# Two stream waits in the gated delta heads of a three-layer kernel

## The chip, the cores and the metric

The kernel runs on one core of one Trainium2 chip. The metric is the device time of one launch in microseconds (us), the median of 3 runs. A core has five engines, each working through its own instructions in order and waiting at semaphores for the others: TensorE (PE, with PEld for its weight loads), VectorE (DVE), ScalarE (ACT), GpSimd (POOL) and SyncE (SP), which here only issues transfers. On-chip memory is SBUF; matrix products land in PSUM.

## The reference, cut to what matters

The program computes a gated delta layer with memory attention and a feed-forward layer, then a convolution layer, a sparse attention layer and two more feed-forward layers, on 512 positions of width 1024. Everything here happens in the first part, the gated delta rule with 8 heads of width 128:

```
q = l2norm(q) * 128**-0.5;  k = l2norm(k);  beta = sigmoid(b)
G = cumsum(g);  decay = exp(G_i - G_j) on and below the diagonal
lower = strictly lower part of beta * (k k^T) * decay
u, w = solve (I + lower) x = [v * beta, k * beta * exp(G)]
p = (q k^T) * decay
per chunk:  v_new = u - w S;  o = (q exp(G)) S + p v_new
            S = S * exp(G_last) + (k exp(G_last - G))^T v_new
o = rms_norm(o) * silu(z)
```

with q, k, v and z the columns of one projection of the normed input, and q, k and v passed through a causal convolution of width 4 and a silu.

## The kernel before, in words

The weights are multiplied in three passes (high x high, high x low and low x high halves of a float32 product, lines 230 to 232), so one projection of a head (128 columns) is 24 matmuls of 512 columns. Weights come from memory through SP's queue in the order of a list, ScalarE rounds them to a high half (L223), and GpSimd forms the low half of the heads' weights (L225).

A head h of the gated delta part is one Python generator, `gdn_head` (L657), and the projections of all heads, then those of the memory attention, are another (`projections`, `gdn_proj` L635). Both are run by the class `Mix` (L88): it keeps a clock and a list of streams, and always takes the stream of least rank that may run. A stream hands back a pair: the first number moves the clock on (estimated TensorE time), the second says for how long that stream steps aside. So `yield 0.0, 5` adds nothing; it lets the others emit up to 5 us of TensorE work before the stream goes on. Heads have ranks 0 to 7, the memory heads 20 and more, and the projections 40, so that they are what fills in. A stream can also hand back a condition. What `Mix` emits is a program order; a list scheduler of the language's runtime then takes it as priorities and fixes for each engine the order in which its instructions stand. That order is final: an engine that waits for one instruction waits with all that follow it.

A head's steps, with the names that the tables use:

- `gdn_proj`: products `wk`, `wq`, `wv`, `wz` of the head (L230 to L232); for k, q and v a scaled copy and three shifted products on VectorE (L644), then a silu on ScalarE (all of ScalarE's functions are recorded at L170); for z only the silu.
- Transposes of k, q, v into PSUM (`natk`, `natq`, `natv`, L668). Of k and q ScalarE takes squares (`sqk`, `sqq`) and VectorE sums (`ss`, L673); of v VectorE forms beta v (`bv`, L676).
- Norms and gates: a logarithm (`lr`), small columns `cs` on VectorE (L681 to L691, of which L685 and L686 form `aL`), two exponentials of them on ScalarE, and `kg`, k times a column (L693).
- Decays: for L and P, transposes of broadcast columns into PSUM (`pbL`, `pbP`, L699), VectorE's differences (`ddL`, `ddP`, L702), an exponential, products of keys and queries (`pkL`, `pkP`, L710) and the elementwise product (L711); for P also `eq` (L707).
- The solve of 16x16 blocks: a mask on GpSimd (`um`, L718), a reduction (`uc`, L720), then 15 steps of shuffle, product and difference (`br`, `xc`, L726 to L728) on VectorE.
- Two levels of combining (`pya`, `pza`, `pyb`, `pzb`, L751, and `py`, `pt`, L776 and L783), four chunks of the recurrence (`pc`, `po`, L796 to L815), a norm of the output (`pr`, `rs`) and its split into halves (`ym`).

Functions of ScalarE come in table sets. Logarithm and exponential share one that the kernel asks for at L162 (`lnexp`); the silu is in another. Where the order puts a function of another set next, a load (ACT_TABLE_LOAD) stands before it.

The steps of the prediction touch the loop at L663 to L677, the gates at L678 to L693 and the decays from L695 on.

Of the kernel before, what the change touches and what calls it, by code (L numbers as in the profile page):

```python
# [125 lines left out]
def body(ctx, tc, I, out, dump=None):  # L126
# [11 lines left out]
    def slot(name, dt=F32):  # L138
        return act.tile([P, S], dt, tag="s", name=name)
# [7 lines left out]
    def bank(name):  # L147
        return psg.tile([P, S], F32, tag="g", name=name)
# [16 lines left out]
    def af(o, i, func, **k):  # L165
        if func in (AF.Ln, AF.Exp):
            lnexp()
        elif func not in (AF.Copy, AF.Square):
            table[0] = func
        return A.activation(o, i, func, **k)  # L170
# [450 lines left out]
    def v4(t):  # L621
        return t.rearrange("p (c i) -> p c i", i=P)

    def bl(t, c):
        return t[:, c * P:(c + 1) * P]

    def cbc(col):
        return col.unsqueeze(2).to_broadcast([P, NB, P])
# [28 lines left out]
    def gdn_head(h):  # L657
# [5 lines left out]
        nat = {}  # L663
        for i, nm in enumerate("kqv"):
            t = kqv[nm]
            ps = bank(f"nat{nm}{h}")
            for c in range(NB):
                T.transpose(bl(ps, c), bl(t, c), ident)  # L668
            nat[nm] = ps
            if nm != "v":  # L670
                s2 = slot(f"sq{nm}{h}")
                af(s2, ps, AF.Square)
                V.tensor_reduce(ss[:, 4 * i:4 * i + 4], v4(s2), AX.X, ALU.add)  # L673
            else:
                bv = slot(f"bv{h}")
                V.tensor_tensor(v4(bv), v4(ps), cbc(beta[:, :, h]), ALU.mult)  # L676
            yield 0.43, 0  # L677
# [13 lines left out]
        V.tensor_scalar(ea, ea, -1.0, None, ALU.mult)  # L691
        kg = slot(f"kg{h}")
        V.tensor_tensor(v4(kg), v4(nat["k"]), cbc(ek), ALU.mult)  # L693

        mats = []  # L695
        for i, (nm, col, mv) in enumerate((("L", aL, kT), ("P", aP, qT))):
# [258 lines left out]
    for h in range(NH):  # L955
        mix.add(gdn_head(h), h)
# [841 lines left out]
```

## Time and profile before

| | |
|---|---|
| median of 3 runs | 2055.21 us (2054.76 to 2057.18) |
| the profiled execution | 2055.91 us, its span 2054.1 us |
| granted TensorE clock, mean | 0.992 |
| PE busy | 1982.7 us (97%) |
| DVE busy | 1543.8 us (75%) |
| ACT busy | 1036.7 us (50%) |
| POOL busy | 321.4 us (16%) |

Busy shares are of the whole span. The gated delta heads fill only the stretch from about 48 to 430 us, and a share over the span says little of it. "Idle before" is the time in which an engine stood still right ahead of an instruction; what is named behind the arrow ended it.

### The profile page before, as it was taken

What the parts mean: (1) busy time and instruction counts of PE and PEld (TensorE: products, weight loads), DVE (VectorE), ACT (ScalarE), POOL (GpSimd) and SP (SyncE); (2) the same over time, 40 slices, a digit from 0 to 9 for tenths busy, and PEclk for the clock granted to TensorE, in tenths of its full rate; (3) what the DMA queues carried; (4) which work ended last, traced back from release to release, by engine and by line L of the source; (5) the groups of instructions that cost most, each with busy time, mean ns of one, the idle gap of its engine ahead of it and who ended that gap; (6) DMA issues with size and microseconds to landing.
All of it is one profiled execution on the core that took longest, in us unless ns stands there. A gap on an engine that the chain in (4) does not pass through costs nothing.

```text
span 2054.1 us, 32051 instructions
## 1 busy us (share of the span) xinstructions
PE 1982.7 (97%) x12464; PEld 1695.7 (83%) x12464; DVE 1543.8 (75%) x2887; ACT 1036.7 (50%) x1734; POOL 321.4 (16%) x227
## 2 busy tenths in 40 slices
PE   7898889999999999998999999999999999999998
PEld 5777777878899988886589999888766678999987
DVE  5888888655989982597778999535888868998832
ACT  5545666553544452457754445434766645444522
POOL 3332433101100000148100000000333310000000
PEclk9999999999999999999999999999999999999999
DMA  5211111412233333233122333334100022323331
GB/s 149 62 52 52 52 52 62 142 55 81 79 107 104 103 113 97 81 92 103 42 93 93 113 101 109 106 95 116 52 22 22 21 65 77 116 93 114 106 99 63
DMA packets 204577, 172.45 MB, mean 84 GB/s; under 512 B 13250, under 2 KB 199243, under 8 KB 204425
## 3 DMA queue, kind: packets, MB, share of 16 engines
q1 hardware_dynamic: 197248, 163.85, 25.9%
q10 hardware_dynamic: 6152, 3.40, 0.6%
q0 software_dynamic: 1024, 3.15, 0.5%
q8 instruction: 98, 1.61, 0.3%
q14 instruction: 55, 0.44, 0.1%
HBM read 165.15 MB, written 2.10 MB: 81 GB/s over the span
## 4 chain that ended last, share of the span: by engine, by line
PE 81%; DVE 14%; ACT 2%; issue 1%; POOL 0%; DMA 0%; ACTq 0%; DVEq 0%; POOLq 0%
PE f L230 16%; PE f L231 16%; PE f L232 16%; PE ao L1676 2%; PE pT L1655 2%; DVE br L727 1%; DVE xc L728 1%; PE cv L1249 1%; PE p L232 1%; PE p L231 1%; PE p L230 1%; DVE dw L1277 1%; PE s L1568 1%; PE wo L231 1%; PE wo L230 1%
## 5 line engine op out<-in xcount | busy, mean ns | idle before, releaser
L225 DVE TENSOR_TENSOR f_l<-f_r,f_h 128x1024 fp32r<-128x1024 f32 (+2 forms) x88 | 101.2, 1151 | 166.8 <-ACT f_h L223 162.9
L223 ACT CAST f_h<-f_r 128x1024 fp32r<-128x1024 f32 (+2 forms) x88 | 87.1, 991 | 188.1 <-PE f L231 148.7
L1646 POOL TENSOR_SCALAR p<-p,dn 128x256 f32<-128x256 f32 (+2 forms) x64 | 72.8, 1142 | 120.5 <-DVE dn L1644 83.6
L170 ACT ACTIVATE p<-s,nm 128x512 f32<-128x512 f32 (+3 forms) x128 | 66.3, 528 | 34.8 <-DVE nm L1640 13.9
L1442 POOL CAST KB<-K 128x128 fp32r<-128x128 f32 x4 | 1.6, 410 | 464.6 <-ACT K L1418 464.6
L170 ACT ACT_TABLE_LOAD x45 | 57.7, 1283 | 12.8 <-DVE v L644 4.9
L359 DVE TENSOR_TENSOR f_s<-f_s,f 128x1024 f32<-128x1024 f32 x52 | 63.5, 1221 | 0.1
L225 POOL TENSOR_TENSOR p_a_l<-p_a_r,p_a_h 128x1024 fp32r<-128x1024 f32 x4 | 9.9, 2474 | 330.3 <-DMA p_a_r<-in_a_pw_w 315.4
L1640 DVE TENSOR_REDUCE nm<-s 128x1 f32<-128x512 f32 (+2 forms) x96 | 50.2, 547 | 7.4 <-PE s L1568 6.8
L354 ACT CAST f_q1h<-f 128x1024 fp32r<-128x1024 f32 x26 | 27.3, 1051 | 55.9 <-DVE f_q3l L355 54.9
L355 DVE TENSOR_TENSOR f_q1l<-f,f_q1h 128x1024 fp32r<-128x1024 f32 x26 | 31.9, 1225 | 25.4 <-ACT f_q1h L354 25.4
L1275 POOL TENSOR_TENSOR dw<-dw,dt 128x511 f32<-128x511 f32 (+29 forms) x30 | 43.7, 1456 | 28.6 <-ACT dt L170 26.8
L225 DVE TENSOR_TENSOR p_l<-p_r,p_h 128x1024 fp32r<-128x1024 f32 x20 | 30.6, 1536 | 18.2 <-ACT p_h L223 18.2
L1655 PEld LDWEIGHTS pT<-cst,p 128*128 128x128 f32 x320 | 36.0, 140 | 9.2 <-issue 4.2
L1676 PE MATMUL ao<-pt,vN 128*64 128x128 f32 (+3 forms) x256 | 42.6, 440 | 0.0
L354 ACT CAST f_q7h<-f 128x1024 fp32r<-128x1024 f32 x26 | 27.3, 1049 | 29.0 <-DVE f_q2l L355 26.6
L354 ACT CAST f_q2h<-f 128x1024 fp32r<-128x1024 f32 x26 | 27.3, 1052 | 27.9 <-issue 27.0
L1655 PE MATMUL pT<-cst,p 128*128 128x128 f32 x320 | 41.1, 274 | 0.2 <-DVE pt L1659 0.2
L727 DVE TENSOR_TENSOR br<-br,uc 128x4 f32<-128x4 f32 (+14 forms) x120 | 38.6, 322 | 2.5
L354 ACT CAST f_q6h<-f_s 128x1024 fp32r<-128x1024 f32 x26 | 27.4, 1052 | 25.6 <-DVE f_s L359 12.7
L354 ACT CAST f_q5h<-f_s 128x1024 fp32r<-128x1024 f32 x26 | 27.3, 1051 | 24.7 <-DVE f_s L359 23.8
L728 DVE TENSOR_TENSOR xc<-xc,br 128x4 f32<-128x4 f32 (+14 forms) x120 | 37.1, 309 | 2.7
(2420 smaller groups left out, 7977.0 us busy)
## 6 DMA issues: line engine op xcount, KB each, us to landing
f<-in_ffn_w_in SPq DMA_DIRECT2D x72, 512.0 KB, 3.9
f<-in_w_ffn_in SPq DMA_DIRECT2D x32, 512.0 KB, 3.5
f_r<-in_ffn_w_out SPq DMA_DIRECT2D x30, 512.0 KB, 3.4
p_r<-in_a_pw_w SPq DMA_DIRECT2D x20, 512.0 KB, 4.0
f_r<-in_w_ffn_out SPq DMA_DIRECT2D x14, 512.0 KB, 3.4
wo_r<-in_w_out SPq DMA_DIRECT2D x12, 512.0 KB, 3.4
f_r<-in_ffn_w_out SPq DMA_DIRECT2D x14, 384.0 KB, 3.0
wk_r<-in_gdn_w_in SPq DMA_DIRECT2D x8, 512.0 KB, 3.7
```

Of the source, the lines that this page charges most:

```text
L170: return A.activation(o, i, func, **k)
L223: A.copy(hi, raw)
L225: (G if idle else V).tensor_tensor(lo, raw, hi.bitcast(F32), ALU.subtract)
L230: T.matmul(ps, wh, xh, start=first, stop=False)
L231: T.matmul(ps, wh, xl, start=False, stop=False)
L232: T.matmul(ps, wl, xh, start=False, stop=last)
L354: A.copy(hi, raw)
L359: V.tensor_tensor(raws[o], raws[a], raws[b], ALU.add)
L727: V.tensor_tensor(br[:, :, 0:w], br[:, :, 0:w], uc[:, :, i:i + 1].to_broadcast([P, NB, w]), ALU.mult)
L1646: (V if br else G).tensor_scalar(pp[br, qb], pp[br, qb], den[:, br:br + 1], None, ALU.mult)
L1655: T.transpose(ps[:, off + (qb - kb) * P:off + (qb - kb + 1) * P], bl(pp[br, qb], kb), ident)
L1676: T.matmul(po[64 * i:64 * i + 64, kb * P:S], VN[br][:, kb * P + 64 * g:kb * P + 64 * g + 64], rhs, start=False, stop=j == 7)
```

## The change: two pairs of numbers

`gdn_head` hands control back twice more: ahead of the transposes of v, for 3.0, and behind `kg`, ahead of the decays, for 2.0. No instruction is named in it.

```diff
         for i, nm in enumerate("kqv"):
             t = kqv[nm]
+            if nm == "v":
+                yield 0.0, 3.0
             ps = bank(f"nat{nm}{h}")
...
         kg = slot(f"kg{h}")
         V.tensor_tensor(v4(kg), v4(nat["k"]), cbc(ek), ALU.mult)
+        yield 0.0, 2.0
```

Lines of the changed kernel stand 2 or 3 further down. The order in which instructions stand is another from the first head on. Counted over the whole program, ScalarE's order has 66 table loads before and 81 now. Of the 15 more, 3 stand up to the silu of head 0's z, 5 between it and that of head 1's z, then 1, 2, 3 fewer, 2, 4 and none for the heads 2 to 7, and 1 behind.

ScalarE, head 1, from the squares of its queries to the exponential of its decays, before:

```order
L162 ACT_TABLE_LOAD
L170 ACTIVATE lr1_736<-ss1_701,epst_86 128x8
L170 ACT_TABLE_LOAD
L170 ACTIVATE v1_681<-v1_681 128x512
L170 ACT_TABLE_LOAD
L170 ACTIVATE cs1_740<-cs1_740 128x4 x2
L223 CAST wz2_3328_0_h_967<-wz2_3328_0_r_966 128x1024
L170 ACTIVATE ddL1_756<-ddL1_756 128x512
```

and now:

```order
L162 ACT_TABLE_LOAD
L170 ACT_TABLE_LOAD
L170 ACTIVATE v1_666<-v1_666 128x512
L170 ACT_TABLE_LOAD
L170 ACTIVATE lr1_744<-ss1_686,epst_86 128x8
L223 CAST wz2_3328_0_h_927<-wz2_3328_0_r_926 128x1024
L170 ACT_TABLE_LOAD
L170 ACTIVATE cs1_748<-cs1_748 128x4 x2
L170 ACT_TABLE_LOAD
L170 ACTIVATE z1_762<-wz10_672 128x512
L170 ACT_TABLE_LOAD
L170 ACTIVATE ddL1_793<-ddL1_793 128x512
```

The silu of v stands ahead of the logarithm, the silu of z ahead of the exponential of the decays (before, it stood behind them), and six loads stand where there were three.

VectorE, where the products of head 2's values (`v2`) stand among the steps of head 1's solve (`br1`, `xc1`, counted down from 15 to 1), before:

```order
L726 STREAM_SHUFFLE br1_3_1041<-xc1_811 128x4x13
L727 TENSOR_TENSOR br1_3_1041<-br1_3_1041,uc1_809 128x4x13
L728 TENSOR_TENSOR xc1_811<-xc1_811,br1_3_1041 128x4x13
L726 STREAM_SHUFFLE br1_2_1069<-xc1_811 128x4x14
L785 TENSOR_SCALAR XU0_913<-pt0_2_1035 64x4x64
L644 SCALAR_TENSOR_TENSOR v2_1019<-wv20_965,vecs_88,v2_1019 128x511
L673 TENSOR_REDUCE ss2_1045<-sqk2_1051 128x4
L644 SCALAR_TENSOR_TENSOR v2_1019<-wv20_965,vecs_88,v2_1019 128x510
L673 TENSOR_REDUCE ss2_1045<-sqq2_1059 128x4
L644 SCALAR_TENSOR_TENSOR v2_1019<-wv20_965,vecs_88,v2_1019 128x509
L727 TENSOR_TENSOR br1_2_1069<-br1_2_1069,uc1_809 128x4x14
```

and now:

```order
L731 TENSOR_TENSOR xc1_849<-xc1_849,br1_4_1012 128x4x12
...
L729 STREAM_SHUFFLE br1_4_1062<-xc1_849 128x4x12
L730 TENSOR_TENSOR br1_4_1062<-br1_4_1062,uc1_847 128x4x12
L731 TENSOR_TENSOR xc1_849<-xc1_849,br1_4_1062 128x4x12
L644 SCALAR_TENSOR_TENSOR v2_994<-wv20_925,vecs_88,v2_994 128x511
L675 TENSOR_REDUCE ss2_1014<-sqk2_1020 128x4
L644 SCALAR_TENSOR_TENSOR v2_994<-wv20_925,vecs_88,v2_994 128x510
L675 TENSOR_REDUCE ss2_1014<-sqq2_1032 128x4
L644 SCALAR_TENSOR_TENSOR v2_994<-wv20_925,vecs_88,v2_994 128x509
L729 STREAM_SHUFFLE br1_3_1076<-xc1_849 128x4x13
```

The products of v stand a step and a third earlier, and the product `XU0` of the head before, which stood ahead of them, is gone from here.

TensorE, around the transposes of head 2's values and its first decays (`wk30` is the projection that fills in, `pc0_0` and `pt0_2` belong to head 0), before:

```order
L231 MATMUL wk30_1187<-u0_1l_174,wk3_1408_0_h_1027 128x512
L668 MATMUL natv2_1062<-cst_80,v2_1019 128x128 x4
L802 MATMUL pc0_0_1077<-bv0_449,XU0_913 128x128
L699 MATMUL pbL2_1096<-cst_80,cs2_1085 128x128 x4
L232 MATMUL wk30_1187<-u0_1h_173,wk3_1408_0_l_1028 128x512
L710 MATMUL pkL2_1107<-k2_880 128x128 x4
```

and now:

```order
L230 MATMUL wk30_1140<-u0_2h_182,wk3_1408_0_h_1006 128x512
L670 MATMUL natv2_1066<-cst_80,v2_994 128x128 x4
L786 MATMUL pt0_2_1103<-XU0_955,y0_2_1060 64x64 x4
L702 MATMUL pbL2_1113<-cst_80,cs2_1084 128x128 x4
L713 MATMUL pkL2_1125<-k2_864 128x128 x4
L805 MATMUL pc0_0_1132<-bv0_464,XU0_955 128x128
```

The transposes of v stand one row later, with two more matmuls of the filler ahead of them; nothing of 3 us has come in between, and `pbL` still follows closely, behind products of head 0. Over the heads 0 to 7 the row number of `natv` on TensorE went from 163, 266, 377, 502, 651, 778, 894, 1012 to 159, 261, 378, 501, 639, 756, 905, 1010, and that of `pbL` from 164, 267, 379, 503, 652, 779, 904, 1023 to 170, 273, 380, 506, 653, 774, 914, 1032.

## Rows read from the trace of the kernel before

**Rows 1.** Busy time of the engines in two stretches of the heads, in us.

```profile
core 0: us, PE busy (x) PEld busy (x) DVE busy (x) ACT busy (x) POOL busy (x), PEclk, DMA share, GB/s
60.00:340.00 280.00, 246.98 (x1374) 204.64 (x1372) 240.91 (x754) 159.56 (x237) 101.54 (x55) 0.96 0.18 53
340.00:400.00 60.00, 58.52 (x390) 51.96 (x391) 45.26 (x139) 32.38 (x62) 15.05 (x18) 0.97 0.35 121
```

**Rows 2.** The chain that ended last, 40 to 410 us: by line, then pieces.

```profile
by line: DVE br L727 7.5%; DVE xc L728 7.4%; DVE v L644 4.3%; DVE br L726 4.1%; DVE q L644 3.7%; issue 3.2%; ACT L170 3.1%; PE pkL L710 2.2%; PE wk L232 2.2%; PE wk L230 2.1%; PE wq L230 2.1%; PE wk L231 2.1%; PE wq L232 2.0%; DVE ss L673 2
...
86.66 0.64 ACT v L170
87.34 1.12 PE natv L668 x4
```

**Rows 3.** TensorE's waits, 60 to 400 us: total us, times, longest.

```profile
PE natv L668 <- ACT v L170: 8.6, 5, 4.0
PE pbL L699 <- DVE cs L686: 4.4, 2, 2.9
PE pbL L699 <- DVE cs L688: 2.0, 1, 2.0
PE natq L668 <- ACT q L170: 1.9, 1, 1.9
PE pkP L710 <- DVE kg L693: 1.3, 1, 1.3
```

**Rows 4.** VectorE's waits for these transposes, 50 to 350 us.

```profile
DVE bv L676 <- PE natv L668: 5.8, 3, 2.6
DVE ddP L702 <- PE pbP L699: 4.4, 4, 1.7
```

**Rows 5.** TensorE in order of time: start, us, [idle before <- releaser].

```profile
87.34 1.12 PE L668 MATMUL natv<-cst,v 128*128 128x128 f32 x4 [4.05 <-ACT v L170]
89.10 1.92 PE L710 MATMUL pkL<-k 128*128 128x128 f32 x8
...
124.62 0.66 PE L668 MATMUL natv<-cst,v 128*128 128x128 f32 x4 [2.34 <-ACT v L170]
126.06 1.16 PE L710 MATMUL pkL<-k 128*128 128x128 f32 x8
...
219.18 0.44 PE L699 MATMUL pbL<-cst,cs 128*128 128x128 f32 x1 [2.91 <-DVE cs L686]
```

**Rows 6.** ScalarE's table loads in the whole span: count, busy us, mean ns.

```profile
L170 ACT ACT_TABLE_LOAD x45 | 57.7, 1283 | 12.8 <-DVE v L644 4.9 <-DVE q L644 4.0 <-DVE k L644 2.4
L162 ACT ACT_TABLE_LOAD x21 | 26.9, 1283 | 1.1 <-PEq L1788 0.7
```

**Rows 7.** ScalarE in order of time, heads 1 and 2.

```profile
87.30 1.28 ACT L170 ACT_TABLE_LOAD   x1
88.60 0.30 ACT L170 ACTIVATE cs<-cs 128x4 f32<-128x4 f32 x2
...
96.10 0.60 ACT L170 ACTIVATE z<-wz 128x512 f32<-128x512 f32 x1
...
123.94 0.63 ACT L170 ACTIVATE v<-v 128x512 f32<-128x512 f32 x1
...
127.55 0.20 ACT L170 ACTIVATE cs<-cs 128x4 f32<-128x4 f32 x1
127.66 1.03 ACT L223 CAST wz_h<-wz_r 128x1024 fp32r<-128x1024 f32 x1
129.72 0.64 ACT L170 ACTIVATE ddL<-ddL 128x512 f32<-128x512 f32 x1 [1.03 <-DVE ddL L702]
```

**Rows 8.** VectorE in order of time, head 2.

```profile
119.00 0.41 DVE L785 TENSOR_SCALAR XU<-pt 64x256 f32<-64x256 f32 x1
...
127.97 0.68 DVE L693 TENSOR_TENSOR kg<-natk,cs 128x512 f32<-128x512 f32 x1
128.57 1.12 DVE L702 SCALAR_TENSOR_TENSOR ddL<-pbL,cs,tab 128x128 f32<-128x128 f32 x4
...
136.66 1.03 DVE L720 TENSOR_REDUCE uc<-um 128x64 f32<-128x512 f32 x1 [0.67 <-POOL um L718]
```

## The prediction

> **What bounds the kernel now.** I read the busy times by stretch first, because the page's shares are means over stages with different limits and the change acts in one stage alone. From 60 to 340 us, where the heads follow one another, TensorE is busy for 246.98 of 280 us and VectorE for 240.91, so TensorE stands still for 33 us and no engine is full; from 340 to 400 us TensorE is busy for 58.52 of 60 [rows 1]. Behind that stretch the change moves nothing but names. VectorE's 240.91 understates it: of a solve step only the product and the difference count, not the shuffle.
>
> The second view is the chain that ended last. Between 40 and 410 us its largest lines are the solve steps on VectorE (7.5 + 7.4 + 4.1% of 370 us, 70 us over 120 steps, so about 0.6 us a step), then VectorE's products for v and q; at a head's start it crosses over, by the silu of v on ScalarE, to the transposes of v on TensorE [rows 2]. So the stage is a loop of engines that wait for each other: VectorE's solve of one head delays the values of the next, TensorE stands at their transposes, and VectorE then waits for what TensorE could not do.
>
> The third view, TensorE's waits, gives the size of what the change is aimed at: 8.6 us for v, 4.4 + 2.0 us for the columns of the decays, 1.3 us for `kg`, together 16.3 us; the queries cost 1.9 [rows 3]. The same stops appear on VectorE as 5.8 and 4.4 us [rows 4]. The longest, 4.05 us in head 1, costs more than itself: behind it the eight matmuls of `pkL` took 1.92 us, in head 2 they took 1.16 [rows 5], which is the lower of the clock's two levels (1.2 against 2.4 GHz) after the engine had stood still.
>
> **The change, part by part.** No instruction is named in it, but ScalarE's order has 15 loads more, 15 x 1.283 = 19.2 us at the duration of the 66 [rows 6]. ScalarE has room: 159.56 of 280 us busy [rows 1]. What counts is where a load stands in a chain.
>
> *Heads 0 and 1.* Eight of the 15 stand here. In head 0 the logarithm, the exponential of the columns and that of the decays each come later by one load or more, so the solve of head 0 starts up to 2.5 us later (two loads). Head 1's q stands behind these solve steps on VectorE, so the 1.9 us wait for q grows by as much at worst. Against that, v of head 1 stands one and two thirds of a step earlier (1.0 us), and the decays' columns have eleven matmuls of filler ahead of them, so TensorE works while they are made. At the end of the decays I find both engines where they were. Bounds -1.0 and +2.5 us; I take +0.5, nearer to the lower because VectorE was waiting there before (5.8 us for `bv`, 2.6 of it here or in head 0) [rows 4].
>
> *Head 2.* Its values stand 1 1/3 steps (0.8 us) and one product `XU` (0.41) [rows 8] earlier on VectorE, so the silu, which ran at 123.94 [rows 7], ends 1.2 us earlier, at 123.4, and `natv` with it. TensorE reaches it earlier too; the 2.34 us wait [rows 5] stays about as it is, but everything is earlier by 1.2. Then one load instead of two leads to both exponentials of the columns: 123.4 + 0.4 for a small copy + 1.28 = 125.1 against 127.55 [rows 7], so `kg` comes 2.5 us earlier than 127.97 [rows 8]. Here the new order takes something back: a rounding of weights (1.03), a load, the silu of z (0.60) and a load (1.28 each) now stand ahead of the decays' exponential, 125.3 + 4.2 = 129.5, only 0.2 earlier than 129.72 [rows 7]. The solve of head 2 (136.66 [rows 8]) starts between 0.2 and 2.5 us earlier; I take 1.5, above the middle, because the row of 136.66 itself waited for GpSimd's mask, whose queue is freed earlier.
>
> *Heads 3 to 7.* Of the 16.3 us, 4.05 and 2.34 belong to heads 1 and 2, and 2.91 to the columns of head 4 [rows 5], where VectorE's and TensorE's places move alike, so that this wait stays. That leaves 7.0 us. Summed from the order with the durations of the trace, the last product for v has 1.6, 2.6, 3.0 and 4.8 us less VectorE work ahead of it in heads 3, 4, 5 and 7 (0.3 more in head 6), and `pbL` has 0.9, 3.1 and 2.7 us more TensorE work ahead in heads 3, 6 and 7. So most of the 7.0 should go. Not all of it is time: VectorE, the other bound, has the same work. Bounds: 0 (it comes back as other waits) and 7.0 + 2.91; I take 5.0.
>
> *The silu of z ahead of the decays*, in all heads but head 3: 2 x 1.28 + 0.60 = 3.2 us of ScalarE between the columns and the decays' exponential. `kg` and the differences (0.68 + 1.12 + as much again = 2.9 us [rows 8]) hide nearly all of it, and in heads 3 to 7 other heads' products stand in between; uncovered it would be 3.2 a head. For heads 4 to 7 together: 0 to 12.8; I take 1.5, near the covered end that those rows give.
>
> What is queued behind the moved waits: TensorE's projections, and through them SP's weight queue, which is not bound here (the DMA share is 0.18 [rows 1]). GpSimd's order keeps its neighbours, except that some masks stand behind one more weight.
>
> Sum: +0.5 - 1.5 - 5.0 + 1.5 = -4.5 us. The profiled execution took 2055.91, so it would be 2051.4; the median of the runs shown is 0.7 lower, so I predict 2050.7.
>
> For the loads, the Trainium skill (ScalarE: Activation LUTs, "What ACT_TABLE_LOAD costs") gives 1283 ns and about 1380 ns more for a drain, 2.66 us a switch, and asks to group functions by set. The trace has the 1283 ns, but no drain behind a load: the one at 87.30 ends at 88.58, and the exponential starts at 88.60 [rows 7]. By the page the 15 loads would be 39.9 us instead of 19.2, and this estimate would put the slower rival below at about twice its price; by the row it stands as given.
>
> **The rivals.**
>
> *The loads decide (slower).* The place is the stretch from the columns to the decays' exponential in the six heads 0, 1, 2, 4, 5 and 6. For it: in heads 0 and 1 VectorE has nothing else between the differences and the product, and the loads come in pairs of which one is wasted. Against it: 2.9 of 3.2 us are covered. The price is 6 x 3.2 = 19 us if nothing covers them, less the 6.5 gained above: +12.5. It decides as soon as more than a third of the 19 shows; I price it at two thirds uncovered, +6 to +8, so 2061 to 2063. Head 7 adds to it: its decays' exponential now stands behind the memory's norm.
>
> *The order hardly moves the waiting (no change).* TensorE's rows of `natv` move by -4, -5, +1, -1 in heads 0 to 3, not by 3 us. VectorE is the bound, TensorE's idle time comes back at the chunks of the recurrence, and only the gain of head 2 against the loss of heads 0 and 1 stays: +0.5 - 1.5 + 1.5, about 2055 to 2056.
>
> *More than the waits goes (much faster).* The clock's mean over 60 to 340 us is 0.96 [rows 1], up to 0.04 x 280 = 11 us at the lower level. If TensorE no longer stands still, half of that goes too: 9.9 + 2.5 + 5.6 - 0.5 - 3.5 = 14, so 2041.
>
> **How the numbers follow.** A measurement of this kernel tells 0.2%, 4.1 us, from no change, so faster is below 2051.1 and slower above 2059.3. The forecast has 0.45 (its own range 2046 to 2054; 0.28 of it below 2051.1), no change 0.18, slower 0.22, much faster 0.15. Faster: 0.28 + 0.15 = 0.43. Within 0.2%: 0.17 + 0.16 = 0.33. Slower: 0.22 + 0.02 = 0.24. The range is 2041 to 2063, the prices of the outer cases; half of each lies outside.
>
> **What would show it.** In the profile of the changed kernel: 81 table loads; TensorE's wait for v below 6 us and for the columns below 4; `natv` of head 1 within 1 us of 87.3, with a longer wait for q ahead of it; the solve of head 2 starting before 136; VectorE's waits for `natv` nearly gone and new ones for the exponential of the decays. The prediction is wrong if TensorE's idle time between 60 and 340 us is still 33 us or more, or if VectorE waits for ScalarE for more than it saved at TensorE.

## The result and the profile after

The changed kernel is slower: a median of 2067.35 us (2065.24 to 2068.95) against 2055.20 for the kernel before on the same chip, a ratio of 1.0059 (95% interval 1.0047 to 1.0071). The forecast was 2050.7, its range ended at 2063. The profiled execution took 2067.55 us with a span of 2065.8, 11.7 longer. Single executions of the kernel before ranged from 2049.98 to 2058.91 us, so times are medians, and a difference of 3 us between the times of two traces says little.

The busy times in the two stretches of [rows 1], and the slice of the second in which the clock fell, changed kernel (engine busy us and instructions, then the granted clock as a share of 2.4 GHz):

```profile
60.00:340.00 280.00, 250.52 (x1389) 208.25 (x1387) 235.30 (x758) 172.09 (x248) 99.17 (x53) 0.95 0.19 53
340.00:400.00 60.00, 54.39 (x298) 46.83 (x298) 37.90 (x132) 25.94 (x50) 15.16 (x19) 0.83 0.28 89
360.00:380.00 20.00, 18.31 (x78) 15.06 (x77) 11.80 (x52) 6.10 (x14) 0.03 (x1) 0.57 0.08 27
```

The same slice in the kernel before:

```profile
360.00:380.00 20.00, 19.77 (x115) 15.90 (x114) 16.44 (x46) 11.12 (x21) 8.25 (x11) 1.00 0.26 85
```

Each row is to be read with two losses: the time in which TensorE stands still, and the time that the lower level (1.2 GHz) takes away, that is one minus the clock, times the length (good to about 1 us over 280, as the clock is given in hundredths). From 60 to 340 us the first fell from 33.0 to 29.5 and the second rose from 11.2 to 14.0: nothing gained. From 340 to 400 us they rose from 1.5 + 1.8 to 5.6 + 10.2, and that is the result: 12.5 us. Over both the stops are 34.5 before and 35.1 after, and the lower clock is 13.0 and 24.2. The slice with the clock of 0.57 looks busy (18.31 of 20) but holds 78 matmuls; the same slice before held 115.

TensorE's waits, 60 to 400 us, answering [rows 3] (total us, times, longest):

```profile
PE natq L670 <- ACT q L170: 4.4, 1, 4.4
PE pt L786 <- ACT y L782: 3.9, 1, 3.9
PE pbL L702 <- DVE cs L688: 3.7, 1, 3.7
PE pc L799 <- DVE S L816: 3.6, 2, 1.9
...
PE natv L670 <- ACT v L170: 0.4, 1, 0.4
```

The 8.6 us for v are down to 0.4. In their place stand q, columns, the state S, and y. VectorE, 50 to 350 us, answering [rows 4]:

```profile
DVE bv L678 <- PE natv L670: 9.7, 5, 3.5
DVE wmk_l L225 <- ACT wmk_h L223: 5.5, 1, 5.5
DVE ddL L714 <- ACT ddL L170: 5.1, 5, 2.0
```

The wait for v has crossed over: TensorE has filler ahead of the transposes and no longer stands, but VectorE's product `bv` stands and waits for them (9.7 against 5.8). The second line belongs to head 7. How it comes about, on ScalarE and then on VectorE in order of time (start, us, [idle before <- releaser]):

```profile
340.34 0.35 ACT L170 ACTIVATE cs<-cs 128x4 f32<-128x4 f32 x2 [3.05 <-DVE cs L688]
340.71 1.28 ACT L170 ACT_TABLE_LOAD   x1
342.00 0.60 ACT L170 ACTIVATE z<-wz 128x512 f32<-128x512 f32 x1
347.14 0.63 ACT L170 ACTIVATE memq<-mem 128x512 f32<-128x512 f32 x1 [4.54 <-DMA mem<-in_mem]
347.67 0.19 ACT L170 ACTIVATION_READ_ACCUMULATOR memq<-mem 128x1 f32 x1
347.76 1.04 ACT L223 CAST wmk_h<-wmk_r 128x1024 fp32r<-128x1024 f32 x1
...
357.32 0.63 ACT L170 ACTIVATE ddL<-ddL 128x512 f32<-128x512 f32 x1 [1.21 <-DVE ddL L705]
```

```profile
341.52 0.68 DVE L695 TENSOR_TENSOR kg<-natk,cs 128x512 f32<-128x512 f32 x1
...
348.83 1.23 DVE L225 TENSOR_TENSOR wmk_l<-wmk_r,wmk_h 128x1024 fp32r<-128x1024 f32 x1 [5.53 <-ACT wmk_h L223]
...
354.15 0.35 DVE L705 SCALAR_TENSOR_TENSOR ddL<-pbL,cs,tab 128x128 f32<-128x128 f32 x1
...
362.23 0.99 DVE L723 TENSOR_REDUCE uc<-um 128x64 f32<-128x512 f32 x1
```

The same two steps of head 7 on VectorE in the kernel before:

```profile
341.79 1.12 DVE L702 SCALAR_TENSOR_TENSOR ddL<-pbL,cs,tab 128x128 f32<-128x128 f32 x4
...
350.06 1.04 DVE L720 TENSOR_REDUCE uc<-um 128x64 f32<-128x512 f32 x1 [1.16 <-POOL um L718]
```

At the columns of head 7 the kernels are level, as TensorE shows (before, then changed):

```profile
340.90 0.62 PE L699 MATMUL pbL<-cst,cs 128*128 128x128 f32 x4 [1.98 <-DVE cs L688]
340.45 0.62 PE L702 MATMUL pbL<-cst,cs 128*128 128x128 f32 x4 [1.65 <-DVE cs L690]
```

Then the memory's norm, which stood behind the decays, stands ahead of them. ScalarE waits 4.54 us for the transfer of `mem`, and the rounding of the memory's weights waits behind it; VectorE waits 5.53 us for that rounding, with the differences of the decays behind it. The solve of head 7 starts at 362.23 instead of 350.06. TensorE uses up its filler (no projection matmul starts between 358.14 and 368.25) and goes on at the lower clock.

### The profile page after: what moved, and what is told of

The parts are those of the page before. It is cut to its first block, busy times and chain, and to the rows that moved or that the text cites. A ratio compares the mean times of both kernels' runs of the same rounds, so it can differ in the third digit from the quotient of the medians.

```text
span 2065.8 us, 32063 instructions
## 1 busy us (share of the span) xinstructions
PE 1993.1 (96%) x12464; PEld 1703.8 (82%) x12464; DVE 1535.8 (74%) x2887; ACT 1054.2 (51%) x1749; POOL 319.3 (15%) x227
## 4 chain that ended last, share of the span: by engine, by line
PE 78%; DVE 10%; ACT 2%; issue 1%; POOL 0%; DMA 0%; ACTq 0%; DVEq 0%; POOLq 0%
PE f L230 16%; PE f L232 16%; PE f L231 16%; PE ao L1679 2%; PE pT L1658 2%; PE cv L1252 1%; PE p L232 1%; PE p L231 1%; PE p L230 1%; DVE dw L1280 1%; PE s L1571 1%; PE wo L230 1%; PE wo L231 1%; PE wo L232 1%; PE s L1569 1%
## 5 line engine op out<-in xcount | busy, mean ns | idle before, releaser
L170 ACT ACT_TABLE_LOAD x55 | 70.6, 1283 | 22.7 <-DVE br L730 7.0
L355 DVE TENSOR_TENSOR f_q1l<-f,f_q1h 128x1024 fp32r<-128x1024 f32 x26 | 31.8, 1225 | 25.1 <-ACT f_q1h L354 25.1
L354 ACT CAST f_q7h<-f 128x1024 fp32r<-128x1024 f32 x26 | 27.3, 1050 | 28.7 <-DVE f_q2l L355 26.2
L354 ACT CAST f_q5h<-f_s 128x1024 fp32r<-128x1024 f32 x26 | 27.3, 1052 | 24.8 <-DVE f_s L359 24.0
L359 DVE TENSOR_TENSOR f_s<-f,f 128x1024 f32<-128x1024 f32 x26 | 31.6, 1215 | 6.0 <-DMA f<-in_ffn_w_in 6.0
```

The costliest lines, as they stand in the source:

```text
L354: A.copy(hi, raw)
L359: V.tensor_tensor(raws[o], raws[a], raws[b], ALU.add)
```

## The experiments

Each table row is one run: table loads, where the memory's norm stands against head 7's decays, the time from `pbL` to `uc` of head 7, TensorE's two losses from 48 to 450 us (stops + lower clock, summed over eleven stretches of the profile), and the ratio to the kernel before on the same chip, 95% interval. "w" is the wait ahead of the values, "d" that ahead of the decays.

| kernel | loads | norm | pbL to uc | stops + clock | ratio |
|---|---|---|---|---|---|
| before | 66 | behind | 9.2 | 34.5 + 12.1 | 1 |
| changed | 81 | ahead | 21.8 | 35.3 + 24.7 | 1.0059 (1.0047, 1.0071) |
| e1 w all, d heads 0-6 | 80 | behind | 8.3 | 34.0 + 15.2 | 0.9999 (0.9990, 1.0007) |
| e2 w, d head 7 only | 68 | ahead | 20.0 | 34.2 + 12.0 | 1.0024 (1.0015, 1.0033) |
| e3 w only | 73 | behind | 8.5 | 36.1 + 17.8 | 1.0030 (1.0018, 1.0042) |
| e4 d only | 65 | behind | 9.1 | 28.5 + 20.5 | 1.0011 (1.0002, 1.0021) |
| e5 mem on SP's queue | 80 | ahead | 20.2 | 35.4 + 22.0 | 1.0048 (1.0036, 1.0060) |
| e6 norm written later | 97 | far behind | 7.2 | 39.6 + 24.2 | 1.0082 (1.0069, 1.0095) |
| e7 before + 16 loads | 81 | behind | 7.3 | 33.5 + 22.2 | 1.0033 (1.0021, 1.0046) |
| e8 w, d heads 0-3 | 79 | behind | 9.5 | 35.6 + 17.5 | 1.0032 (1.0019, 1.0044) |
| e9 before, z copied | 65 | behind | 7.2 | 33.0 + 19.6 | 1.0017 (1.0008, 1.0027) |
| e10 e1, z copied | 60 | behind | 9.1 | 36.0 + 19.3 | 1.0037 (1.0023, 1.0051) |
| e11 changed, z copied | 60 | ahead | 21.6 | 38.7 + 22.8 | 1.0066 (1.0052, 1.0080) |
| e12 before, norm in head 6 | 67 | in head 6 | 7.0 | 39.9 + 15.5 | 1.0046 (1.0031, 1.0060) |
| e13 w 2.0, d 2.0 | 79 | between L and P | 21.6 | 40.9 + 23.5 | 1.0095 (1.0080, 1.0111) |
| e14 w 5.0, d 2.0 | 65 | ahead | 20.0 | 31.9 + 27.3 | 1.0058 (1.0045, 1.0070) |
| e15 w 1.0, d 1.0 | 64 | behind | 6.5 | 38.4 + 15.8 | 1.0042 (1.0029, 1.0054) |
| e16 changed + work in stops | 81 | ahead | 21.6 | 31.8 + 14.3 | 1.0028 (1.0018, 1.0038) |
| e17 before + work in stops | 70 | behind | 7.4 | 34.3 + 15.0 | 1.0038 (1.0025, 1.0052) |
| e18 e1 + work in stops | 78 | behind | 9.7 | 30.3 + 11.6 | 1.0019 (1.0010, 1.0029) |

The losses are those of the one profiled execution, the ratio that of all. In the runs that add no work for TensorE, the two losses together, less the 46.6 us of the kernel before, agree to about 3 us with what their profiled execution took above its 2055.91. The column from `pbL` to `uc` falls into two groups, 6.5 to 10 and 20 to 22 us, and only the place of the norm divides them.

**Undoing one part: e1 and e2.** The edit of e1 (e2 has `h == 7` at both waits):

```diff
-        yield 0.0, 2.0
+        if h < 7:
+            yield 0.0, 2.0
```

e1, expected: 

> Both waits in heads 0 to 6, in head 7 only the one ahead of the values. ScalarE's order has 80 table loads (81 in the changed kernel, 66 before), but the memory's norm stands behind the exponentials of head 7's decays again, as before the change. Theory 'tail' (what is lost is the 12.2 us by which the first reduction of head 7's solve, uc, starts later, 362.2 against 350.1 us): 2052 to 2057 us, the loss of 12 us gone, uc of head 7 at 348 to 352 us. Rival 'loads' (the 15 loads more set the time): one load fewer changes nothing, 2065 to 2069 us.

e2, expected: 

> Both waits in head 7 alone, heads 0 to 6 as before. ScalarE's order has 68 table loads; the memory's norm stands ahead of the exponentials of head 7's decays. Theory 'tail': the whole loss or a little more, 2065 to 2070 us, with VectorE waiting about 5 us for the first rounding of the memory's weights (wmk_h) and ScalarE about 4 us for the transfer of mem. Rival 'loads': 2 loads more are 2.6 us, 2055 to 2058 us.

e1 took 2057.0 us against 2056.12: the loss is gone with 80 of the 81 loads still there, and `uc` of head 7 is back at 352.0. That refutes "loads" as the cause of the result, and by this pair one wait in one head carries the whole 0.6%. e1's stretches:

```profile
60.00:340.00 280.00, 250.38 (x1385) 208.42 (x1384) 232.75 (x753) 172.68 (x248) 96.77 (x52) 0.95 0.19 53
340.00:400.00 60.00, 55.57 (x369) 48.75 (x368) 45.98 (x146) 28.96 (x60) 17.96 (x20) 0.97 0.35 115
360.00:380.00 20.00, 18.44 (x108) 14.75 (x107) 17.26 (x54) 11.04 (x22) 7.45 (x10) 1.00 0.19 54
```

In the first row TensorE's busy time is the changed kernel's but for 0.14 us, with the same clock, and the ratio is 1, so the other waits together are worth nothing: neither the forecast gain nor a loss. e2 took 2060.45 us: the norm alone does cost, but 4 to 5 us, not 12; the expectation missed. `uc` came nearly as late behind the columns (20.0), but the lower clock from 340 to 400 us took 5.4 us (0.91) instead of 10.2. Its stretches:

```profile
60.00:340.00 280.00, 249.12 (x1414) 207.35 (x1412) 242.92 (x763) 163.73 (x245) 103.05 (x57) 0.98 0.19 55
340.00:400.00 60.00, 56.70 (x342) 49.47 (x342) 40.60 (x128) 29.90 (x56) 12.73 (x15) 0.91 0.33 108
```

The trace of e2 shows something else. Up to 329 us TensorE, VectorE, ScalarE and GpSimd run their instructions in the order of the kernel before, and up to 144 us TensorE's matmuls start within 0.3 us of each other; then the clock falls in one execution and not in the other (kernel before, then e2):

```profile
144.00:147.00 3.00, 3.00 (x12) 2.62 (x12) 2.81 (x13) 0.63 (x1) 0.00 (x0) 0.50 0.00 1
144.00:147.00 3.00, 3.00 (x18) 2.60 (x18) 2.76 (x13) 0.61 (x1) 0.00 (x0) 1.00 0.05 11
```

With a second such place at 170 us e2 stands 3.5 us ahead by 200 us. So one order can differ by 3.5 us from execution to execution through the clock. e2's profiled execution was its shortest (2057.23); from the columns of head 7 (3.6 ahead, at 337.30) to the end of its span (1.4 behind) it lost 5.0 us, about what the median says.

**One wait at a time: e3 and e4.** The edits take out one of the two lines of the change.

e3, expected: 

> Only the wait of 3.0 ahead of the values, in all heads. 73 table loads, the memory's norm behind head 7's decays. Theory 'tail': no loss, 2050 to 2057 us. Rival 'loads': half of the loads, half of the loss, 2060 to 2062 us.

e4, expected: 

> Only the wait of 2.0 ahead of the decays, in all heads. 65 table loads, one fewer than before, the memory's norm behind head 7's decays. Theory 'tail': no loss, 2050 to 2057 us. Rival 'loads': 2054 us, one load less than before. Both agree here; the run tells what the second wait alone is worth in the heads.

2062.84 and 2059.17 us. e3 fits neither theory: "tail" allowed no loss with the norm behind, and the rival's number (2060 to 2062) nearly came, but the loss lies between 260 and 340 us, where TensorE waits 3.9 us for y and 3.1 for `rs`. e4 is a little above its range. Neither wait gains alone.

**The transfer and the place: e5 and e6.**

```diff
-            mn = rows_normed("mem", I["mem"], 2, nc.gpsimd)
+            mn = rows_normed("mem", I["mem"], 2, nc.sync)
```

e5, expected: 

> The changed kernel with the four transfers of mem issued on SP's queue instead of GpSimd's; ScalarE's and VectorE's orders stay but for a few neighbours, and the memory's norm still stands ahead of head 7's decays. It takes away what the squares of mem wait for (4.54 us on ScalarE: the transfers stand on GpSimd's queue behind the masks of head 6's solve). Theory 'tail' in two parts (the wait for the transfer about 5, the norm's own work ahead of the decays about 7): 2060 to 2063 us, VectorE's 5.5 us wait for wmk_h gone. If the place alone decides and not the transfer: 2066 to 2068 us.

2065.81 us. VectorE's wait for `wmk_h` fell from 5.5 to 0.2, but another took its place at once (VectorE's waits, 335 to 380 us):

```profile
DVE memq L548 <- DMA mem<-in_mem: 3.9, 2, 3.0
DVE XU L788 <- PE pt L786: 2.6, 1, 2.6
DVE mem L565 <- ACT memr L170: 2.5, 1, 2.5
```

On SP's queue the transfers stand behind weights and started at 343.30 against 344.05, so this run hardly took the transfer away; a version with `mem` loaded long before was not built. In e2 ScalarE's first squares of `mem` waited for nothing at 340.32, its second for 0.5 us and VectorE's for 2.0 and 0.3, and the solve came 20.0 us behind the columns all the same: the place delays it even where the transfer hardly does.

```diff
+        yield from dense_g("wqm", xs, pairs(4112, 4), ev_qm)
         with tc.issue_after(marks[5]):
             mn = rows_normed("mem", I["mem"], 2, nc.gpsimd)
-        yield from dense_g("wqm", xs, pairs(4112, 4), ev_qm)
```

e6, expected: 

> The changed kernel, all waits kept, with the memory's norm written behind the memory's query projection instead of ahead of it. The norm stands behind head 7's decays and solve, and ScalarE's order has 97 table loads. Theory 'tail': 2053 to 2058 us although 16 loads more are in it. Rival 'loads': above 2067 us, up to 16 x 1.28 = 20 us more.

2072.96 us, a miss. Head 7 is no longer delayed (7.2), but TensorE now waits 7.2 us for the normed `mem` (`mt`) and 5.1 for columns. The norm can be too late as well as too early; this run doesn't separate that from the 16 loads.

**The loads: e7, and e9 to e11.** e7 pins two loads ahead of the decays' exponential of the kernel before:

```diff
+            if i == 0:
+                for st in ("silu_and_others", "natural_log_exp_and_others"):
+                    tc.keep_in_program_order(A.preload_act_table_set(st))
             af(dd, dd, AF.Exp)
```

e7, expected: 

> The kernel before with two loads more in each head, right between the exponential of the columns and that of the decays: 81 loads as in the changed kernel, 157 of 11,198 rows of TensorE's order moved. It measures the term that the prediction put at +1.5 us for four heads. Theory 'tail' (the loads are covered by kg and the differences): 2055 to 2059 us. Rival 'loads': 8 x 2.57 = 20 us uncovered, at two thirds 2068 to 2072 us.

2063.22 us, +7.1 and between the two: 20.5 us of loads at this place show to a third. That speaks against the covered end, on which the term of the prediction was set: by this run eight loads (four heads) would cost 3.6, not 1.5. But 157 rows of TensorE's order moved as well, and other kernels with moved rows and fewer loads lost 0.2 to 0.4% (e9, e15), so 7.1 us is not shown to be the price of the loads. Its loads in the whole span, and its stretches (the last is where it lost most):

```profile
L705 ACT ACT_TABLE_LOAD x16 | 20.5, 1283 | 0.2
```

```profile
60.00:340.00 280.00, 250.36 (x1332) 208.06 (x1330) 230.42 (x734) 166.72 (x240) 98.56 (x53) 0.92 0.17 50
340.00:400.00 60.00, 56.17 (x359) 48.19 (x360) 49.75 (x154) 36.68 (x65) 21.16 (x21) 1.00 0.34 115
142.00:162.00 20.00, 19.18 (x70) 16.85 (x71) 9.91 (x42) 3.06 (x6) 5.57 (x4) 0.57 0.15 43
```

From 60 to 340 us TensorE's stops did not grow (29.6 against 33.0); the clock fell from 0.96 to 0.92, which is 11 us of 280. From 142 to 162 us the clock was 0.57, as in the changed kernel's tail.

e9 to e11 take the loads for z out of three kernels (the silu of z becomes a copy, which leaves that part of the computation out):

```diff
-                af(t, ps if nm == "z" else t, AF.Silu)
+                af(t, ps if nm == "z" else t, AF.Copy if nm == "z" else AF.Silu)
```

e9, expected: 

> The kernel before with a plain copy in place of the silu of z (this part of the computation is changed): 65 table loads instead of 66, the order around it as before. Base for the next two. Both theories: 2053 to 2058 us.

e10, expected: 

> The first experiment's kernel (both waits in heads 0 to 6, in head 7 the first alone) with a plain copy in place of the silu of z: 60 table loads instead of 80, the waits and their order kept. Rival 'the loads eat what the waits give' (7.1 us for 16 loads, 0.44 each, 14 to 20 loads): 2046 to 2051 us. Theory 'the waiting returns elsewhere on TensorE' (columns, the state and y instead of v): 2054 to 2058 us, as its base.

e11, expected: 

> The changed kernel with a plain copy in place of the silu of z: 60 table loads, the memory's norm ahead of head 7's decays as in the changed kernel. Against the run with 60 loads and the norm behind them it prices the place alone. Theory 'tail': 10 to 13 us above that run. Rival (the loads inside the norm's chain make its price): at most 6 us above it.

2059.42, 2062.48 and 2067.72 us. e9 and e10 lie above all of their ranges. With fewer loads than their base the waits are still no gain (e10 against e9: +3.1), so the loads were not what ate it. The norm's place costs 5.2 (e11 against e10), under the expected 10 to 13 and inside the rival's "at most 6". The rival's reason does not show, though: with 60 loads the solve stands as far behind the columns (21.6) as with 81. e9 is a warning: one load fewer and an order nearly that of before, and yet 0.17% slower, with more lower clock in its trace (19.6 against 12.1).

**Other places and amounts: e8, e12 to e15.** e8 has `h < 4` at both waits; e12 writes the norm ahead of head 7's projections; e13 to e15 change the amounts.

e8, expected: 

> Both waits in heads 0 to 3 only. 79 loads, the memory's norm behind head 7's decays. In the changed kernel TensorE lost 5.8 us less than before by 200 us and 7.9 more from 200 to 300. If that later loss belongs to the waits of heads 4 to 6: 2048 to 2053 us. If heads 0 to 3 gain nothing that lasts: 2054 to 2059 us.

e12, expected: 

> The kernel before with the memory's norm written ahead of head 7's projections, so that it stands ahead of the decays' product of head 6's neighbourhood and is over before head 7's decays. 67 table loads. If the norm costs by delaying a solve wherever it stands ahead of one: 2058 to 2066 us. If it finds room there and head 7 gains the ScalarE time: 2050 to 2055 us.

e13, expected: 

> The changed kernel with 2.0 instead of 3.0 ahead of the values, all heads, nothing else. The memory's norm stands behind head 7's decays, ScalarE's order has 79 table loads (81 in the changed kernel). Theory 'tail': 2055 to 2060 us. Rival 'loads': 2064 to 2067 us.

e14, expected: 

> The changed kernel with 5.0 instead of 3.0 ahead of the values, all heads. The memory's norm stands ahead of head 7's decays, and the order has 65 table loads, one fewer than before. Theory 'tail' (4 to 12 us for the norm's place in the runs so far): 2060 to 2068 us. Rival 'loads': 2053 to 2057 us.

e15, expected: 

> The changed kernel with 1.0 and 1.0 instead of 3.0 and 2.0. The memory's norm stands behind head 7's decays, 64 table loads: neither of the two suspected costs. If short waits keep what TensorE's wait for the values gives: 2048 to 2054 us, faster than both kernels. If the order of the heads gives nothing by itself: 2054 to 2059 us.

e8 (2060.89 us) gained nothing that lasts; it lies above both ranges. e12 (2065.13, in the range for a norm that costs wherever it stands) holds up a combining step instead of a solve: TensorE waits 4.7 us at `pzb` for VectorE's part of the norm, and the columns of head 7 come at 354.18. e14 (2066.91) has one load fewer than the kernel before and the whole loss, with a clock of 0.66 from 360 to 380 us. e13 (2074.49) was expected among the kernels with the norm behind, which misread its order: only the exponential of L stands ahead of it, that of P behind. VectorE in e13:

```profile
363.66 1.23 DVE L225 TENSOR_TENSOR wmk_l<-wmk_r,wmk_h 128x1024 fp32r<-128x1024 f32 x1 [3.71 <-ACT wmk_h L223]
...
372.11 1.23 DVE L225 TENSOR_TENSOR wmk_l<-wmk_r,wmk_h 128x1024 fp32r<-128x1024 f32 x1 [3.17 <-ACT wmk_h L223]
...
375.24 1.04 DVE L723 TENSOR_REDUCE uc<-um 128x64 f32<-128x512 f32 x1
```

So it belongs with the others, two waits for `wmk_h` ahead of the solve; but it was 12.8 us behind already at the columns of head 7 (353.65), so the norm is not all of its 0.95%. e15 (2064.17) has neither of the suspected costs and is 0.42% slower all the same; both expectations missed. Its TensorE stands 7.1 us for v and 7.3 for columns.

**The clock: e16 to e18.** Matmuls into a bank that the next product overwrites, so that TensorE has work in a stop. e16:

```diff
             ps = bank(f"{name}{h}")
+            for _ in range(6 if h == 6 and name != "pya" else 0):
+                T.matmul(ps, xs[0][0][:, 0:P], xs[0][0], start=True, stop=True)
```

e16, expected: 

> The changed kernel with 18 matmuls more on TensorE (six of 128x512 each ahead of pza, pyb and pzb of head 6, into the bank that these then overwrite), 4 us of work at the full clock. In the changed kernel TensorE worked at a mean granted clock of 0.57 from 360 to 380 us, 8.5 us lost, behind a stop at 361.5 to 363.6. If most of the tail's price is that clock and work in the stop keeps it up: 2060 to 2065 us. If the price is the waiting for the late solve of head 7, or the clock falls all the same: 2067 to 2072 us.

2061.88 us, 5.5 less than the changed kernel with 18 matmuls more. VectorE starts the solve of head 7 as late as there (362.04), and from 60 to 360 us every instruction that both traces have starts within 0.4 us of its fellow; then (VectorE's row, two of the added groups on TensorE, and the stretch):

```profile
362.04 1.02 DVE L723 TENSOR_REDUCE uc<-um 128x64 f32<-128x512 f32 x1
```

```profile
359.95 1.66 PE L754 MATMUL pza<-u_0h 128*128 128x512 f32 x6
...
362.70 1.62 PE L754 MATMUL pyb<-u_0h 128*128 128x512 f32 x6
```

```profile
360.00:380.00 20.00, 19.68 (x127) 16.64 (x127) 17.73 (x72) 9.20 (x19) 0.00 (x0) 1.00 0.16 50
```

The clock stays at 2.4 GHz where the changed kernel had 0.57. Projection matmuls follow each other at 0.23 us, so the additions are 4.1 us of work. From 340 to 400 us the stops fell from 5.6 to 2.1 us and the loss at the lower clock from 10.2 to nothing, and the profiled execution (2058.67) is 8.9 us shorter. So in these traces most of the tail's price is the lower clock behind the late solve, not the waiting for it. By the medians the price of the clock is less certain, between 5.5 us and, if the additions cost their full 4.1, 9.6 of the 12: the executions of e16 that took 2060.44 us or more have a mean clock of 0.988 to 0.990, the profiled one 0.991. The Trainium skill (TensorE: Matmul & The Clock Gate, "What's actually happening") calls the lower level the default state, which activity releases; e16 agrees, with 0.57 against 1.00 for the same stretch without and with the added work.

e17 puts such work (six matmuls, and transposes of `lr`) ahead of `pyb` of head 0 and `pbL` of heads 3, 4 and 7 in the kernel before; e18 ahead of five stops of e1.

e17, expected: 

> The kernel before with work for TensorE right ahead of four of its stops, overwritten by what follows: six matmuls of 128x512 ahead of pyb of head 0, and eight transposes of broadcast columns (of lr, ready before cs) ahead of pbL of heads 3, 4 and 7. In the kernel before the stretches behind these stops (144 to 148, 166 to 176, 218 to 224, 342 to 346 us) were at the lower clock and lost 8.5 us. If filling a stop keeps the clock, as in the last run: 2047 to 2053 us. If the added work costs what it gives: 2055 to 2060 us.

e18, expected: 

> The first experiment's kernel (both waits in heads 0 to 6, in head 7 the first alone) with work for TensorE right ahead of five stops: natq of head 1 (stop of 4.4 us), pyb of head 1 (2.2), pbL of head 5 (3.6) and of head 7 (1.7), pt of head 5 (4.0). The stretches behind them lost 8.5 us at the lower clock. If filling keeps the clock: 2048 to 2053 us, faster than both kernels. If not: 2056 to 2062 us.

2063.34 and 2058.46 us: no gain. In e18 the two losses are 41.9 us, 7.3 less than in e1, and the added work takes it back (22 matmuls at 0.23 and 16 transposes, of which eight took 1.06: about 7 us). One of its places was not the one named: the stop of 4.0 us at `pt` is head 4's, while the matmuls went ahead of `pt` of head 5, where there was no stop. In e17 new stretches at the lower clock appear where none was filled (254 to 262, 288 to 294 us). No version beat the kernel before.

## Why the prediction was wrong

*What bounds the kernel* was read rightly: a loop of engines that wait for each other. What it missed is that the loop's losses are of two kinds, and that the clock's, 13.0 of 47.5 us by [rows 1], can grow; it named the clock only as something to gain, in a rival. One reading was wrong: VectorE's 240.91 us do count the shuffles (L726, 20.0 us of them), so it understates nothing.

*The loads:* 81, as counted, 1283 ns each, and no drain shows behind a load (one ends at 88.96, `lr` starts at 88.98):

```profile
87.68 1.28 ACT L170 ACT_TABLE_LOAD   x1
88.98 0.30 ACT L170 ACTIVATE lr<-ss,epst 128x8 f32<-128x8 f32 x1
```

*Heads 0 and 1 (+0.5, bounds -1.0 and +2.5):* the upper bound came. The wait for q grew from 1.87 to 4.38, as the worst case said, `natv` of head 1 stood at 87.72 and waited 0.43, and the solve of head 1 started 2.5 us later (100.7 against 98.2).

*Head 2 (-1.5):* `natv` at 123.22 without a wait, the solve at 134.49 against 136.66, 2.2 earlier. Right, a little better: the two terms together forecast 1.0 earlier here.

*Heads 3 to 7 (-5.0, then +1.5 for the silu of z):* this step failed first. The waits for v went, as it said, and for a while the time came: the solves of heads 4 and 5 started 5.4 and 4.5 us earlier (223.82 and 264.66). By the solve of head 6 it was gone (2.1 late, 310.49). From the solve of head 2 (2.2 ahead) to the columns of head 7 (0.45 ahead) the kernel lost 1.7 us instead of gaining 3.5. The waits came back in other places: for VectorE at `bv` (9.7), for TensorE at the columns of head 5 (3.7) and at y (3.9). That last one stands where the lead was lost, between the solves of heads 5 and 6, and shows what a silu in between does. ScalarE, changed kernel:

```profile
278.07 0.69 ACT L170 ACTIVATE rs<-pr,epst 128x512 f32<-128x512 f32 x1
278.78 1.28 ACT L162 ACT_TABLE_LOAD   x1
282.32 1.28 ACT L170 ACT_TABLE_LOAD   x1 [2.25 <-DVE q L644]
283.61 0.63 ACT L170 ACTIVATE q<-q 128x512 f32<-128x512 f32 x1
284.26 1.28 ACT L162 ACT_TABLE_LOAD   x1
285.56 0.63 ACT L170 ACTIVATE rs<-rs 128x512 f32<-128x512 f32 x1
...
290.12 0.62 ACT L203 CAST ym3h<-rs 128x512 fp32r<-128x512 f32 x1 [3.00 <-DVE rs L833]
290.77 0.37 ACT L782 COPY y<-py 64x256 f32<-64x256 f32 x1
```

Between the logarithm and the exponential of `rs` stand three loads and the silu of a q, and the copy of y is queued behind all of it. TensorE at the same time, the product for y and what needs the copy:

```profile
277.73 0.68 PE L779 MATMUL py<-X,ddL 64*64 64x64 f32 x8
...
291.19 1.11 PE L786 MATMUL pt<-XU,y 64*64 64x64 f32 x8 [3.94 <-ACT y L782]
```

The product for the y of head 4 lay ready for 12 us. TensorE had run out of the filler that stood ahead of `pt` at 287.3 us. The rival "the order hardly moves the waiting" (chance 0.18) is what came of the heads up to 6, and e1 gives its size: a ratio of 0.9999.

*Head 7:* the step that decided has no term in the sum. The prediction saw that "its decays' exponential now stands behind the memory's norm", but put it as an addition to the rival of the loads, without a price. It wrote that GpSimd's order keeps its neighbours; but the four transfers of `mem` stood behind the mask of head 7 before (349.98 us, the mask at 348.32) and stand ahead of it now (344.05, the mask at 358.76). Following its own rule, it would have named what the norm waits for (these transfers, behind the masks of head 6) and what is queued behind it on VectorE. By the ratios the norm's place cost 12 us in the changed kernel (against e1); in two other pairs it was 4 to 6 (e2, e11 against e10), so its size by itself is not fixed.

*The rivals:* "the loads decide" had the sign and nearly the time (2061 to 2063), with the wrong cause: e1 has 80 loads and no loss, e14 has 65 and all of it. Its price (two thirds of the loads' time uncovered) was about twice the third that e7 shows at most, the forecast's (an eighth) less than half of it. "More than the waits goes" took the clock for something that only gains; it lost 11.2 us more from 60 to 400 us.

*What would show it:* five of its marks came (81 loads, TensorE's wait for v below 6, `natv` of head 1 within 1 us behind a longer wait for q, the solve of head 2 before 136, VectorE's new wait for the decays' exponential, 5.1 us). Two failed: the columns (5.3 us with both lines, not below 4) and VectorE's waits for `natv`, which grew. The test "TensorE idle for 33 us or more from 60 to 340" did not fire (29.5) although the gain was nought: it left the clock out. The other test fired: from 50 to 350 us VectorE's waits for ScalarE, summed over the whole view, rose from 12.5 to 23.1 us, while its waits for TensorE fell only from 24.3 to 22.3.

What stays open: why kernels with neither the norm ahead nor more loads (e15, e9) are 0.2 to 0.4% slower. Their profiles put it on more stops (e15: 38.4 us) or the lower clock (e9: 19.6), but no single instruction was shown to cause it, and e2's trace shows that two executions of one order can stand 3.5 us apart. Since orders without the norm ahead cost up to 0.46%, part of the 12 us between the changed kernel and e1 may be chance of that kind. Also, why nearly the same delay of head 7 met 10.2 us of lower clock in the changed kernel and 5.4 in e2; e2 had filler for longer (its projection matmuls pause from 358.96 to 363.33 us, the changed kernel's from 358.14 to 368.25), but no run tested that.

## What to carry to other kernels

A wait in a stream lets whatever comes next in the program in ahead of the stream's own next step, so look what that is at the end of each loop: here it was another stage's norm, with a transfer in front, ahead of the last head's critical chain. Add up TensorE's losses as stops plus (1 - granted clock) x length; a change that only moves stops about can lose by the second term. Before counting on a wait that goes, write down which wait is next on each of the engines; in a loop of engines near balance it takes its place.

## What was not expected of the hardware

Long stretches at the lower clock in which TensorE shows as busy: 0.57 over 20 us with TensorE busy for 18.3 (78 matmuls, tail of the changed kernel) and 19.2 us (70 matmuls, e7). Work added ahead of and in the stop before one kept the clock at 1.00 and made the kernel 5.5 us faster with 4.1 us more to do. One order of instructions, up to 329 us, took 3.5 us less in one execution than in another, and from 144 to 147 us the clock was 1.00 in the one and 0.50 in the other behind the same instructions (e2 and the kernel before). And the time follows small changes of order: across kernels with the norm behind or elsewhere and 60 to 80 loads, the ratio went from 0.9999 to 1.0046.
